# Two passes over the weights of a hybrid diffusion trunk, rewritten as one pass over all 1536 tokens

## Chip, cores, metric

The kernel runs as one program on the 8 cores of one Trainium2 chip. Every core holds the same weights and works on its own 512 context tokens (two requests of 256) and its own 1024 latent tokens (one request); nothing is exchanged between cores. The metric is the device time of the slowest core in microseconds (us).

Executions come in two states. In the slow state the cores of one die, sometimes of both, have a lower granted clock and the time is longer. (A die is four of the cores; the granted clock is the share of its full clock that TensorE was given, as the profile records it. The fast state is the one without this.) Times below are compared in the fast state, unless it says otherwise.

## The reference, cut to what matters

```python
D_MODEL = 2048; DEPTH = 2; NA_HEADS = 8; NA_HEAD_DIM = 64; D_FF = 8192

def trunk_layer(x, cond, ctx_kv, ...):
    m = jax.nn.silu(cond) @ w_ada + b_ada                 # modulation: six vectors of 2048
    sh1, sc1, g1, sh2, sc2, g2 = split(m, 6)
    h = rmsnorm(x, norm1_g) * (1 + sc1) + sh1
    q, k, v, u, vg, xf, xp, gl = split(h @ w_in)          # 7 x 512 columns, and 4 x 2048 of gates
    q = rmsnorm(q); k = rmsnorm(k)                        # per head
    a = attention                                         # context: dense, 256 keys
                                                          # latent: 8 x 16 neighbourhood + 512 cached keys
    branches = (a, spatial_gating(u, vg), fourier_mix(xf), multiscale_pool(xp))
    merged = sum_i sigmoid(gl_i + b_gate_i) * (branches[i] @ w_branch[i])
    x = x + g1 * (merged @ w_out)
    h2 = rmsnorm(x, norm2_g) * (1 + sc2) + sh2
    x = x + g2 * (square(relu(h2 @ w_mlp1)) @ w_mlp2)
# context tokens go through both layers, latent tokens go through both layers;
# they meet nowhere: the latent tokens read cached keys and values given as inputs.
```

Context and latent tokens use the same weights. A weight tile is 2048 rows by 128 columns: 1 MB in HBM as float32, 512 KB in SBUF as bf16, and 16 matmuls of 128x128 weights for each block of 512 tokens. A layer has 252 such tiles and 96 more for the modulation. Tiles are counted below as 1 MB each (504 tiles are 504 MB); the profile's HBM figures count millions of bytes, 1.05 for a tile.

## The kernel before

It runs the two groups one after the other: first the 1024 latent tokens through both layers, then the 512 context tokens. Each group loads every weight tile. The residual stays in SBUF as float32. (Cuts are marked with `...`.)

```python
    def linear(self, piece_fn, n_out, in3, in_key, NT, consumer, lookahead=1):
        for oc in range(n_out):
            bs = self.load_w(piece_fn(oc))            # one tile, DMA with a cast to bf16
            for tt in range(NT):                      # NT = 2 (latent) or 1 (context)
                bank = self.tr.bank()
                self.mm_group(self.PS[bank][:, :], bs, ...)     # 16 matmuls
                consumer(oc, tt, bank)
            self.ada_tick()
...
    def rsqrt_inplace(self, R, key):
        tr.op('act', lambda e: e.activation(out=R, in_=R, func=AF.Sqrt), ...)
        tr.op('dve', lambda e: e.reciprocal(R, R), ...)
...
        def qk_consumer(which):                       # after each projection of q and k:
                tr.op('dve', ... tensor_copy(qf[:], PS))
                tr.op('act', ... Square)
                tr.op('pe',  ... matmul(BD64, sq))    # sum over the head
                tr.op('dve', ... + EPS)
                self.rsqrt_inplace(R[:], ('sm', 1))
                tr.op('dve', ... qf * gain * R)
                tr.op('act', ... copy to bf16)
                tr.op('pe',  ... matmul(PERM, ...))   # latent: rotary
                ...                                   # three more on 'dve'
...
    def attn_latent(self, l, T, W3, B3, VL, VC, KC, TAB):
        for j in range(4):
            for hh in range(2):
                self.build_bias(l, h, TAB)            # DMA, 14 float32 matmuls, 7 VectorE instructions
                for rp4 in range(2):
                    ...                               # scores, exp, values of one head
...
    def build(self):
        self.phase0()                                 # all 96 modulation tiles of layer 0
        for gi, g in enumerate((1, 0)):               # latent, then context
            self.load_x(g, T)                         # 128x128 transposes through PSUM
            for l in range(DEPTH):
                self.norm_mod(l, g, 0, T)
                self.attention(g, l, T)
                tr.barrier()
                self.gmlp(g, l, T)
                tr.barrier()
                self.fourier(g, l, T)
                tr.barrier()
                self.pool(g, l, T)
                tr.barrier()
                self.merge(l, T)
                self.w_out_phase(l, g, T)
                self.norm_mod(l, g, 1, T)
                self.mlp(l, g, T)
            self.store_y(g, T)
```

Of the kernel before, what the change touches and what calls it, by code (L numbers as in the profile page):

```python
# [11 lines left out]
D = 2048  # L12
DEPTH = 2
# [6 lines left out]
PAST = 512  # L20
# [4 lines left out]
NDMA = 16  # L25
GELU_C = 1.5957691216057308

TRUST_SAME = ('pe',)

class Tracker:  # L30
    def __init__(self, nc):
        self.nc = nc
        self.eng = {'pe': nc.tensor, 'act': nc.scalar, 'dve': nc.vector,
                    'pool': nc.gpsimd, 'sp': nc.sync}
        self.sem = {}
        self.cnt = {}
        self.nsem = 0
        self.waited = {e: {} for e in self.eng}
        self.last_w = {}
        self.readers = {}  # L40
        for e in ('pe', 'act', 'dve', 'pool'):
            self._new_sem(e)
        self.dma_sems = [nc.alloc_semaphore(f"dq{i}") for i in range(NDMA)]
        self.dma_cnt = [0] * NDMA
        self.dma_last = [None] * NDMA
        self.dma_rr = 0
        self.dma_rr_sp = 0
        self.bank_rr = 0
        self.held = set()
        self.all_tokens = {}  # L50
# [5 lines left out]

    def epoch(self):
        for e in ('pe', 'act', 'dve', 'pool'):
            if self.cnt[e] > 0:
                self._new_sem(e)  # L60

    def bank(self, hold=False):
        for _ in range(8):
            b = self.bank_rr
            self.bank_rr = (b + 1) % 8
            if b not in self.held:
                break
        else:
            raise RuntimeError("no free PSUM bank")
        if hold:  # L70
            self.held.add(b)
        return b

    def release(self, b):
        self.held.discard(b)
# [9 lines left out]
    @staticmethod  # L85
    def _expand(keys):
        out = []
        for k in keys:
            if isinstance(k, tuple) and len(k) == 2 and k[0] == 'sm':
                out.append(('smh', k[1], 0))  # L90
                out.append(('smh', k[1], 1))
            else:
                out.append(k)
        return out

    def _deps(self, reads, writes):
        deps = []
        for k in reads:
            t = self.last_w.get(k)
            if t is not None:  # L100
                deps.append(t)
        for k in writes:
            t = self.last_w.get(k)
            if t is not None:
                deps.append(t)
            r = self.readers.get(k)
            if r:
                deps.extend(r.values())
        return deps

    def _record(self, tok, reads, writes):
        for k in reads:
            self.readers.setdefault(k, {})[tok[0].num] = tok
        for k in writes:
            self.last_w[k] = tok
            self.readers[k] = {}
        self.all_tokens[tok[0].num] = tok

    def op(self, e, fn, reads=(), writes=()):
        reads = self._expand(reads)  # L120
        writes = self._expand(writes)
        for tok in self._deps(reads, writes):
            if tok[2] == e and e in TRUST_SAME:
                continue
            self._wait(e, tok)
# [3 lines left out]
        tok = (self.sem[e], self.cnt[e], e)  # L129
        self._record(tok, reads, writes)  # L130
        return tok

    def dma(self, q, fns, reads=(), writes=()):
        reads = self._expand(reads)
        writes = self._expand(writes)
        half = NDMA // 2
        if q == 'sp':
            i = self.dma_rr_sp
            self.dma_rr_sp = (i + 1) % half
        else:  # L140
            i = half + self.dma_rr
            self.dma_rr = (self.dma_rr + 1) % half
        if self.dma_last[i] is not None:
            self._wait(q, self.dma_last[i])
        for tok in self._deps(reads, writes):
            self._wait(q, tok)
        for fn in fns:
            fn(self.eng[q]).then_inc(self.dma_sems[i], 16)
            self.dma_cnt[i] += 16
        tok = (self.dma_sems[i], self.dma_cnt[i], 'dma')  # L150
        self.dma_last[i] = tok
        self._record(tok, reads, writes)
        return tok

    def barrier(self):
        toks = list(self.all_tokens.values())
        for e in self.eng:
            for tok in toks:
                self._wait(e, tok)
        self.last_w = {}  # L160
        self.readers = {}

    def finish(self):
        for tok in list(self.all_tokens.values()):
            self._wait('sp', tok)

def _bf(x):
    return np.ascontiguousarray(x.astype(ml_dtypes.bfloat16))

def make_consts():  # L170
    c = {}
    ident = np.eye(128, dtype=np.float32)
    ones = np.ones((128, 128), np.float32)
# [4 lines left out]
    for m in range(128):  # L178
        d = m % 64
        half = (d % 32) // 16  # L180
        partner = m + 16 if half == 0 else m - 16
        perm[partner, m] = 1.0
    c['cb'] = _bf(np.concatenate([ident, ones, bd, perm], axis=1))
    jf = np.zeros((128, 64), np.float32)
    jf[np.arange(64), 63 - np.arange(64)] = 1.0
    c['cf'] = np.ascontiguousarray(np.concatenate([ident, jf], axis=1))
# [4 lines left out]
    for p in range(128):  # L191
        d = p % 64
        a = d // 32
        half = (d % 32) // 16
        i = d % 16
        ang = (pos[a] * inv[i]).astype(np.float32)
# [3 lines left out]
    qc = np.arange(64)  # L200
    cs = np.clip(qc - 8, 0, 48)
    kc = np.arange(64)
    ok = (kc[:, None] >= cs[None, :]) & (kc[:, None] < cs[None, :] + 16)
    m = np.where(ok, 0.0, NEG).astype(np.float32)
    c['mask2'] = np.concatenate([m, m], axis=0)
# [26 lines left out]

class Builder:
    def __init__(self, debug=None, depth=DEPTH, groups=(1, 0), stage=99, plan=None):
        self.stage = stage
        self.sub = 99
        self.plan = plan
        self.scopes = False
        self.ada_bg = None
        self.ada_tick_n = 0  # L240
        self.wmode = 'plain'
        self.issue_gidx = 0
        self.tile_gidx = {}
        self.rec_tiles = []
        self.rec_segs = []
        self.dma_issued = 0
        self.cast_issued = 0
        self.tile_fs = {}
        self.tile_bs = {}
        self.tile_nk = {}  # L250
        self.seg_i = 0
        self.debug = debug or []
        self.depth = depth
        self.groups = groups
# [5 lines left out]
        self.wtile_idx = 0  # L260
        self.cast_rr = 0

    def decl_dram(self):
# [3 lines left out]
        self.x_in = [di("x0", (512, D)), di("x1", (1024, D))]  # L267
        self.ck = di("ck", (DEPTH, NH, PAST, HD))
        self.cv = di("cv", (DEPTH, NH, PAST, HD))
        self.cond = di("cond", (2, D))  # L270
        self.norm1_g = di("norm1_g", (DEPTH, D))
        self.w_in = di("w_in", (DEPTH, IN_COLS // 128, 128, 2048))
        self.b_gate = di("b_gate", (DEPTH, 4 * D))
        self.q_norm_g = di("q_norm_g", (DEPTH, HD))
        self.k_norm_g = di("k_norm_g", (DEPTH, HD))
        self.rpb_pad = di("rpb_pad", (64 + DEPTH * NH * 15 * 31 + 64,))
        self.gmlp_norm_g = di("gmlp_norm_g", (DEPTH, BW))
        self.w_spatial = di("w_spatial", (DEPTH, 4, 128, 128))
        self.b_spatial = di("b_spatial", (DEPTH, 4 * 128))
        self.w_pool = di("w_pool", (DEPTH, 4, 128, 128))  # L280
        self.pool_scale = di("pool_scale", (DEPTH, BW))
        self.w_branch = di("w_branch", (DEPTH, 4, NCH, 128, 512))
        self.w_out = di("w_out", (DEPTH, NCH, 128, 2048))
        self.norm2_g = di("norm2_g", (DEPTH, D))
# [3 lines left out]
        self.b_ada = di("b_ada", (DEPTH, 6 * D))  # L288
        self.c_cb = di("cb", (128, 512), BF16)
        self.c_cf = di("cf", (128, 192))  # L290
        self.c_rope = di("rope", (128, 2, 1024))
        self.c_mask2 = di("mask2", (128, 64))
        self.c_fcc = di("f_cc", (128, 256), BF16)
        self.c_fn = [di("f_n0", (128, 2, 2, 256), BF16), di("f_n1", (128, 2, 8, 1024), BF16)]
        self.c_pm = di("pm", (128, 4, 5, 128), BF16)
        self.y_out = [do("y0", (512, D)), do("y1", (1024, D))]
        self.nk = do("nk", (2, DEPTH, NH, 256, HD))
        self.nv = do("nv", (2, DEPTH, NH, 256, HD))
        self.wcache_l = [nc.dram_tensor(f"wcache{l}", [300, 128, NCH * 128], BF16, kind="Internal").ap() for l in range(DEPTH)]
        self.dbg = {}  # L300
        for name, shape in self.debug:
            self.dbg[name] = do("dbg_" + name, shape)

    def alloc(self):
        nc = self.nc
        S = nc.alloc_sbuf_tensor
        self.XT = S("XT", [128, NCH * 1024], F32)
        self.HT = S("HT", [128, NCH * 1024], BF16)
        self.WK = S("WK", [128, NCH * 1024], BF16)
        self.BR = S("BR", [128, NCH * 1024], BF16)  # L310
# [25 lines left out]
    def psb(self, b):  # L336
        return self.PS[b][:].bitcast(BF16)
# [1102 lines left out]
```

## Time and profile before

Five runs: 7851, 7852, 7858, 7918 and, in the slow state, 8672 us. The profiled execution was in the slow state (8091 us), but only on one die: cores 0 to 3 spent about 1500 us at clock 0.81, cores 4 to 7 none, and these took 7828 to 7839 us. I read core 5, one of the undisturbed ones.

The page of core 5 of before: busy time of each engine, then tenths of busy time in 40 equal slices for TensorE (PE), its granted clock and the DMA engines, then the HBM traffic.

```profile
PE 6246.0 (80%) x33157; PEld 3025.1 (39%) x33157; DVE 1806.0 (23%) x2586; ACT 1320.3 (17%) x2201; POOL 1248.9 (16%) x1940
...
PE   1244566899799996467799979999469899579899
...
PEclk9966567999899998656999989999779999779999
DMA  9832457445345442101245524443539888359887
...
HBM read 1296.79 MB, written 16.78 MB: 168 GB/s over the span
```

The three rows show three kinds of time. In the first two slices the DMA is full and TensorE nearly idle. In others TensorE is at 4 to 7 tenths and its clock is mostly at 5 to 7: it waits, and it is cold (at half clock) for part of the time. In the rest it is full at full clock. In the full slices of the last quarter (the context pass) the DMA is nearly full too, 8 to 9 tenths.

Busy time of each engine in stretches that are stages of before, core 5. Columns: the stretch in us from the start, its length, then busy us and instruction count of TensorE, its weight loads, VectorE, ScalarE and GpSimd; granted clock, share of the DMA engines, GB/s.

```profile
core 5: us, PE busy (x) PEld busy (x) DVE busy (x) ACT busy (x) POOL busy (x), PEclk, DMA share, GB/s
0.00:331.00 331.00, 56.26 (x1541) 49.92 (x1541) 1.44 (x6) 1.51 (x2) 63.50 (x124) 1.00 0.96 154
...
445.00:1072.80 627.80, 318.97 (x3008) 224.44 (x3009) 204.20 (x336) 138.63 (x265) 52.46 (x82) 0.60 0.34 56
1072.80:1408.50 335.70, 217.21 (x1740) 115.36 (x1740) 78.37 (x116) 66.00 (x110) 43.72 (x79) 0.76 0.67 120
1408.50:1965.60 557.10, 555.86 (x2567) 251.56 (x2568) 156.07 (x229) 89.48 (x129) 68.18 (x129) 1.00 0.50 78
2075.70:2136.70 61.00, 19.17 (x46) 4.82 (x46) 30.79 (x37) 41.38 (x66) 0.25 (x1) 0.60 0.05 9
2136.70:3021.50 884.80, 884.00 (x4082) 400.05 (x4082) 96.09 (x128) 78.32 (x133) 200.38 (x256) 1.00 0.49 76
5852.10:6132.40 280.30, 278.49 (x1280) 125.64 (x1280) 77.49 (x112) 45.36 (x65) 68.18 (x129) 0.99 0.98 149
6219.90:6677.80 457.90, 447.35 (x2050) 201.27 (x2050) 48.06 (x64) 40.14 (x68) 134.77 (x192) 0.99 0.88 146
```

In order these are: the modulation of layer 0; projections and attention of the latent group in layer 0; its spatial gating, Fourier and pooling; its merge; its second norm; its MLP; and of the context pass the merge and the MLP of layer 0. The merge and MLP rows are TensorE from end to end: 4096 matmuls in 884.8 us are 216 ns for each 128x512 matmul. The Trainium skill, "TensorE: Matmul & The Clock Gate", Part 1, gives 215.7 ns for this shape warm; the trace agrees. The attention row is busy for half of its time, and at clock 0.60.

What fills the other half: the timeline of before, core 5, around one projection of q (start, length, engine and line, instruction, outputs and inputs; in brackets the idle time before it and what ended that).

```profile
561.17 0.69 DVE L680 COPY SM<-PS 128x512 f32<-128x512 f32 x1 [2.90 <-PE PS L395]
562.07 0.63 ACT L682 ACTIVATE SM<-SM 128x512 bf16<-128x512 f32 x1 [6.83 <-DVE SM L680]
562.95 0.38 PE L685 MATMUL PS<-SM,CB 128*128 128x512 bf16 x1 [1.96 <-ACT SM L682]
...
564.23 0.63 ACT L596 ACTIVATE SM<-SM 128x512 f32<-128x512 f32 x1 [1.53 <-DVE SM L687]
564.96 3.35 DVE L597 RECIPROCAL SM<-SM 128x512 f32<-128x512 f32 x1 [0.82 <-ACT SM L596]
...
570.12 0.59 PE L710 MATMUL PS<-WK,CB 128*128 128x512 bf16 x1 [6.79 <-ACT WK L693]
...
570.98 5.21 PE L395 MATMUL PS<-HT,WF 128*128 128x512 bf16 x12
```

TensorE follows VectorE and ScalarE through one chain of nine steps: the next projection's matmuls (L395) come after the rotary matmul (L710), and that waited 6.79 us. The largest single piece is the reciprocal, 3.35 us.

### The profile page before, as it was taken

How to read it: one execution, taken by the hardware profiler on the slowest of the kernel's cores; microseconds unless marked ns; L12 is line 12 of the kernel's file. 1: busy time of each engine (PE TensorE's matmuls, PEld its weight loads, DVE VectorE, ACT ScalarE, POOL GpSimd, SP SyncE). 2: the span in 40 equal slices, each digit the busy share in tenths (PEclk: the TensorE clock that was granted, in tenths of full speed). 3: DMA queues.
4: the chain of work that ended last, by engine and by line, in shares of the span. 5: the costliest groups of instructions: out<-in, count | busy, mean ns of one | idle time of the engine just before them, and what ended most of it. 6: DMA issues, size and time to landing. Idle time of an engine off the chain costs nothing.

```text
span 8089.9 us, 91572 instructions; the slowest of 8 cores (7827.5 to 8089.9 us)
## 1 busy us (share of the span) xinstructions
PE 6504.8 (80%) x33157; PEld 3086.8 (38%) x33157; DVE 1806.3 (22%) x2586; ACT 1318.8 (16%) x2201; POOL 1249.0 (15%) x1940
## 2 busy tenths in 40 slices
PE   1244556999799994477999799995698997699899
PEld 1212533444344441263444344443243442244344
DVE  0134240222211113432222211104222103222101
ACT  0121321111200012142111200002212001211100
POOL 2100011111122210000111122221021221011221
PEclk9866567999899996658999899997689987678788
DMA  9822365444344441112455355545288975278675
GB/s 150 162 52 39 60 109 114 75 78 82 54 77 76 77 75 34 15 18 52 67 76 82 53 78 76 77 69 125 49 134 135 146 124 86 47 119 135 102 124 111
DMA packets 213748, 690.37 MB, mean 85 GB/s; under 512 B 24976, under 2 KB 57856, under 8 KB 209984
## 3 DMA queue, kind: packets, MB, share of 16 engines
q0 software_dynamic: 213312, 684.52, 50.6%
q8 instruction: 278, 4.55, 0.2%
q14 instruction: 158, 1.29, 0.1%
HBM read 1296.79 MB, written 16.78 MB: 162 GB/s over the span
## 4 chain that ended last, share of the span: by engine, by line
PE 75%; DMA 7%; DVE 7%; ACT 6%; issue 3%; POOL 0%; ACTq 0%; DVEq 0%; POOLq 0%
PE PS L395 68%; DVE SM L597 2%; DMA WF<-w_ada 2%; DMA HT<-w_ada 2%; PE PS L856 1%; DMA WB<-w_ada 1%; PE PS L1134 1%; ACT WK L948 1%; DMA SM<-rpb_pad 1%; ACT HT L590 1%; DVE SM L587 1%; PE PS L958 1%; ACT SM L574 1%; PE PS L576 1%; DMA WK<-f_n 0%
## 5 line engine op out<-in xcount | busy, mean ns | idle before, releaser
L395 PE MATMUL PS<-HT,WF 128*128 128x512 bf16 x7424 | 1750.8, 398 | 45.4 <-ACT HT L590 34.4
L395 PE MATMUL PS<-HT,WB 128*128 128x512 bf16 x5632 | 1340.5, 400 | 60.4 <-ACT HT L590 34.5
L395 PEld LDWEIGHTS PS<-HT,WF 128*128 128x128 bf16 x7424 | 752.8, 102 | 1001.6 <-issue 301.5
L395 PE MATMUL PS<-WK,WF 128*128 128x512 bf16 x4000 | 902.7, 389 | 9.0 <-POOL WK L1301 4.8
L395 PEld LDWEIGHTS PS<-HT,WB 128*128 128x128 bf16 x5632 | 573.6, 102 | 794.8 <-issue 275.1
L1309 DVE SCALAR_TENSOR_TENSOR XT<-PS,MV,XT 128x512 f32<-128x512 f32 x384 | 288.3, 751 | 2536.2 <-PE PS L395 2536.2
L395 PE MATMUL PS<-WK,WB 128*128 128x512 bf16 x2896 | 656.7, 389 | 11.5 <-POOL WK L1301 9.5
L1299 ACT ACTIVATE SM<-PS 128x512 f32<-128x512 f32 x384 | 229.3, 597 | 2230.3 <-PE PS L395 2230.3
L395 PEld LDWEIGHTS PS<-WK,WF 128*128 128x128 bf16 x4000 | 398.2, 100 | 506.4 <-issue 114.2
L1301 POOL TENSOR_TENSOR WK<-SM 128x512 bf16<-128x512 f32 x384 | 396.6, 1033 | 1064.4 <-ACT SM L1299 1064.4
L395 PE MATMUL PS<-HT 128*128 128x512 bf16 x1920 | 501.0, 426 | 44.2 <-ACT HT L590 41.4
L1241 ACT ACTIVATE SM<-PS,VT 128x512 bf16<-128x512 f32 x384 | 263.9, 687 | 1454.6 <-PE PS L395 1454.5
L395 PEld LDWEIGHTS PS<-WK,WB 128*128 128x128 bf16 x2896 | 288.8, 100 | 373.1 <-issue 88.0
L1258 DVE TENSOR_TENSOR SM<-PS,SM 128x512 f32<-128x512 f32 x288 | 199.1, 691 | 948.6 <-ACT SM L1241 663.8
L395 PEld LDWEIGHTS PS<-HT 128*128 128x128 bf16 x1920 | 205.0, 107 | 326.2 <-issue 255.7
L360 POOL DMA_DIRECT2D WF<-w_mlp x236 | 131.9, 559 | 631.4 <-PE PS L395 609.5
L395 PE MATMUL PS<-WK,HT 128*128 128x512 bf16 x784 | 202.6, 427 | 4.6 <-POOL WK L1301 4.6
L574 ACT ACTIVATE SM<-XT 128x512 bf16<-128x512 f32 x192 | 112.0, 623 | 544.0 <-PE PS L576 472.8
L710 PE MATMUL PS<-WK,CB 128*128 128x512 bf16 x32 | 18.7, 585 | 217.5 <-ACT WK L693 217.5
L576 PE MATMUL PS<-SM,CB 128*128 128x512 bf16 x192 | 95.4, 522 | 121.2 <-ACT SM L574 115.7
L597 DVE RECIPROCAL SM<-SM 128x512 f32<-128x512 f32 x54 | 181.1, 3353 | 49.9 <-ACT SM L596 49.9
L395 PE MATMUL PS<-BR,WF 128*128 128x512 bf16 x772 | 192.2, 388 | 0.0
(193 smaller groups left out, 4544.6 us busy)
## 6 DMA issues: line engine op xcount, KB each, us to landing
WF<-w_mlp POOLq DMA_DIRECT2D x236, 512.0 KB, 5.6
WB<-w_mlp POOLq DMA_DIRECT2D x183, 512.0 KB, 5.7
WF<-w_in POOLq DMA_DIRECT2D x174, 512.0 KB, 5.7
WB<-w_in POOLq DMA_DIRECT2D x129, 512.0 KB, 5.3
HT<-w_mlp POOLq DMA_DIRECT2D x93, 512.0 KB, 5.6
WF<-w_ada POOLq DMA_DIRECT2D x90, 512.0 KB, 11.4
WB<-w_ada POOLq DMA_DIRECT2D x69, 512.0 KB, 10.3
HT<-w_in POOLq DMA_DIRECT2D x65, 512.0 KB, 5.9
```

Source lines behind the costliest of these rows:

```text
L360: self.tr.dma('pool', [lambda e: e.dma_start(out=wb[:, 0:nk, :], in_=src)], writes=[bkey])
L395: ins = e.matmul(out_ap, wb[:, kc, wcol], rhs_fn(kc), start=(n == 0), stop=(n == len(kcs) - 1))
L574: tr.op('act', lambda e, sq=sq, c=c: e.activation(out=sq, in_=X3[:, c, ts], func=AF.Square), reads=[('x', c, tt)], writes=[('smh', 0, c % 2)])
L576: tr.op('pe', lambda e, sq=sq, c=c: e.matmul(self.PS[bank][:, :], self.ONES, sq, start=(c == 0), stop=(c == NCH - 1)), reads=[('smh', 0, c ...
L587: tr.op('dve', lambda e, tmp=tmp, c=c, a_col=a_col: e.scalar_tensor_tensor(tmp[:], X3[:, c, ts], a_col, R[:], ALU.mult, ALU.mult), reads=[ ...
L590: tr.op('act', lambda e, tmp=tmp, c=c, b_col=b_col: e.activation(out=H3[:, c, ts], in_=tmp[:], func=AF.Identity, bias=b_col, scale=1.0), r ...
L597: tr.op('dve', lambda e: e.reciprocal(R, R), reads=[key], writes=[key])
L1241: tr.op('act', lambda e: e.activation(out=gt, in_=self.PS[bank][:, :], func=AF.Sigmoid, bias=bcol, scale=1.0), reads=[('ps', bank), 'VT'], ...
L1258: tr.op('dve', lambda e: e.tensor_tensor(tmp[:], self.PS[bank][:, :], gt, ALU.mult), reads=[('ps', bank), gk], writes=[('sm', 4)])
L1299: tr.op('act', lambda e: e.activation(out=r[:], in_=self.PS[bank][:, :], func=AF.Relu), reads=[('ps', bank)], writes=[rk])
L1301: tr.op('pool', lambda e: e.tensor_tensor(W3[:, oc, ts], r[:], r[:], ALU.mult), reads=[rk], writes=[('wk', oc, tt)])
L1309: tr.op('dve', lambda e: e.scalar_tensor_tensor(X3[:, oc, ts], self.PS[bank][:, :], gcol, X3[:, oc, ts], ALU.mult, ALU.add), reads=[('ps', ...
```

## The change

The intent: go over the weights once for all 1536 tokens (three blocks of 512); keep activations feature-major (features on partitions, tokens along the free dimension) from the input on, so that no block is transposed on TensorE; keep the residual in HBM, since three blocks of it don't fit beside the activations; compute attention for two heads at a time with keys on partitions, so that the softmax's sum comes out of the value matmul; and interleave: a small scheduler with ticks issues the next pair's projections between attention steps and runs norms behind matmuls. The bias tables are index lookups of an input and are now gathered on the host. It is a rewrite: 1172 lines added, 1261 removed. Its core, cut:

```diff
-    def barrier(self):
-        toks = list(self.all_tokens.values())
-        for e in self.eng:
-            for tok in toks:
-                self._wait(e, tok)
...
+    def w_pump(self, need=0):
+            if m >= self.w_low + NSLOT:               # ring of 8 tiles, freed in order
+                return
+            self.tr.dma('pool', self.WBT[:, off:off + 2048], src, writes=[('wb', m % NSLOT)])
...
+    def tick(self, n=1):
+            self.clock += 1
+            while self.deferred and self.deferred[0][0] <= self.clock:
+                self.deferred.pop(0)[2]()
+            for bg in list(self.bgs):                 # norms in the background
+                ...
...
-        tr.op('act', lambda e: e.activation(out=R, in_=R, func=AF.Sqrt), reads=[key], writes=[key])
-        tr.op('dve', lambda e: e.reciprocal(R, R), reads=[key], writes=[key])
+            self.act(R.ap, self.PS[b2][:, :], AF.Ln, [('ps', b2), 'EPS'], [R], bias=self.EPSC)
+            self.act(R.ap, R.ap, AF.Exp, [R], [R], scale=-0.5)
...
+    def fill(j):                                      # what runs between the steps of pair j
+            if j < 3:
+                yield from self.qk_all(l, j + 1, DB)
+            t = self.w(self.w_in[l, 20 + j])          # a quarter of the Fourier projection
+            ...
+        for n in range(N + 2):
+            if n >= 2:
+                values(n - 2)
+            if n < N:
+                scores(n)
+                want = -(-(n - i0 + 1) * tot // nj)
+                while done < want:
+                    next(filler, None)                # 8 matmuls
+                    done += 1
+                    self.tick()
...
+    def one(oc, tt, t):                               # output projection
+            bank = self.bank()
+            self.run(self.group(self.PS[bank][:, :], bank, self.fm(t, self.W3, tt)))
+            x = self.x2(oc, tt)                       # loaded from HBM three tiles ahead
+            self.stt(x.ap, self.PS[bank][:, :], g, x.ap, ALU.mult, ALU.add, ...)
+            tr.dma('sp', self.xa[l][tt, oc], x.ap, ...)
+            self.stat(x, banks[tt], oc, 2)            # sum of squares for the next norm
...
     def build(self):
+        self.phase0()                                 # 32 modulation tiles, not 96
+        for l in range(DEPTH):
+            self.stage_a(l)                           # gating, first pair's q and k, v
+            self.attention(l)
+            self.stage_b(l)                           # Fourier, pooling
+            if l == 0:
+                self.ada_begin(0, [((32, 16),), ((48, 16),), ((64, 16),)])
+            self.merge(l)
+            self.project_out(l)
+            if l == 0:
+                self.ada_begin(0, [((80, 16),)])
+                self.ada_begin(1, [((16 * k, 16),) for k in range(6)])
+            self.mlp(l)
```

## The prediction

It was written from before's profile and the code, with nothing built.

> **What bounds the kernel now.** I read the undisturbed die (core list: cores 4 to 7, 7828 to 7839 us, no throttle; the other die spent about 1500 us at clock 0.81). Busy times by stage (core 5) show two regimes.
>
> - Dense stages are at TensorE's pace: the latent merge (1408-1964 us) is 554.5 of 556 us busy, the two MLP quarters-loops (2140-3020, 4600-5483 us) 880 of 880: one 128x512 matmul per 216.6 ns at clock 1.00. The context pass (5700 on) is at the same pace while its DMA share is 0.86 to 0.89: it reads a 1 MB weight tile for only 16 matmuls (3.47 us).
> - Elsewhere TensorE waits. First 331 us: 96 modulation tiles, DMA share 0.96, TensorE busy 56 us. Loading x and norm, 109 us; each later norm about 62 us (busy 22). Query/key/value 312 us (busy 140), latent attention 320 and 235 us, clock 0.50. The clock record has about 1850 us at half clock.
>
> **The sum after.** The linear layers keep their count: per layer and 512 tokens 252 weight tiles x 16 = 4032 matmuls, so 24192 in all x 216.6 ns = 5240 us. This is the floor and does not shrink. Other TensorE work, from columns at the pace of the dense stages (estimates): attention 126, Fourier 72, norm sums 42, pooling, spatial and query/key helpers 50, modulation 192 tiles x 0.53 us = 100. Sum 5630 us.
>
> Waits that stay (estimates):
> - start: 32 modulation tiles instead of 96, at 3.4 us each, plus x: 135 us, then 20 us while the norms of the latent blocks catch up;
> - attention: per head pair, ScalarE has 40 exponentials x 0.61 us + 20 us of query/key norm and finish = 44 us, VectorE 36, TensorE 49 incl. the next pair's projections: I expect 62-66 us, the last pair about 40, so 135 us of waits in both layers;
> - query/key helpers not covered by one chunk 24; norm sums issued slightly early 30; stage changes and Fourier/pool 60.
>
> 5630 + 135 + 20 + 135 + 24 + 30 + 60 = about 6035 us at clock 1.00; a little throttle gives **6110 us** (ratio 1.29). Gone: barriers, transposes, the 3.35 us reciprocals (54 + 12, now Ln/Exp), 500 MB of the weight reads (HBM read 1297 to about 810 MB; residual traffic adds 100). The gain is mostly idle and cold time, not bytes: the halved weight traffic frees only the start of the context pass, which was hardly slower than TensorE.
>
> **Clock.** The Trainium skill, "TensorE: Matmul & The Clock Gate", Part 1, says that idle windows halve the clock and that three busy cores of a die can bring 13/16. This trace has both: 0.50 in attention, 0.81 on die 0. Filling gaps should end most cold time; denser work can trip the second more often. A throttle over a quarter of the run costs some 300 us, over all of it 1200.
>
> **Range** 5880 to 6600 us. Faster by over 2%: 0.97; within: 0.02; slower: 0.01.
>
> **What would show it.** TensorE busy over 93%; half clock under 400 us; matmul count near 27500 + 3072 small ones; stages: merge 835 us, MLP 1335 us per layer, attention 230 us per layer, dense work starting at 150 us; DMA share well under 0.6 after the start; HBM read about 800 MB.
>
> **What would make it wrong.** A 0.81 clock through the whole run; ScalarE table loads between Ln and softmax Exp (the skill's "ScalarE: Activation LUTs", Table sets, puts both in one set, so I expect few loads; each took 1.28 us here); attention running at over 90 us per pair because in-order ScalarE and VectorE queues block the two score banks; weight DMAs stuck behind a waiting load on the same queue.

## More of the kernel before

The chain of waits of before, core 5, at the start of one head of attention (start, length, what it was):

```profile
797.37 0.48 POOL SM L847
798.08 7.49 DMA SM<-rpb_pad
805.81 5.43 PE PS L856 x25
...
812.20 0.62 DVE BR L860
```

This is layer 0. Each of its 8 heads begins with its bias table: a DMA of 7.5 to 10.3 us during which neither TensorE, VectorE nor ScalarE works, then float32 matmuls of 5.4 us. The DMA engines are at 0.90 in that stretch: modulation tiles of layer 1 are loading at the same time. In layer 1, where no modulation tiles pass, only the first head waits for this DMA (4.4 us), the others for the matmuls alone; a head takes 27 us there and 38 us in layer 0. That the modulation tiles make the difference was not tested.

## The result

Five runs: 6038, 6039, 6039, 6047 and, in the slow state, 6348 us; the median is 6039.4. In the same rounds before had a median of 7857.8. The ratio is 0.7676 (95% interval 0.7637 to 0.7715). Ratios are computed as the mean time of one kernel's fast runs over that of the other's fast runs of the same rounds, so they are not quite the ratio of the medians. The output was correct.

The page of core 7 of after, the slowest core of a fast execution, with the same rows as above:

```profile
PE 5699.3 (94%) x29080; PEld 2582.4 (43%) x29080; DVE 1428.7 (24%) x2172; ACT 1194.6 (20%) x1929; POOL 383.1 (6%) x722
...
PE   1788999999999999999999889999999999999999
...
PEclk9899999999999999999999999999999999999999
DMA  9522144443656578656765221222236334543353
...
HBM read 861.59 MB, written 79.69 MB: 156 GB/s over the span
```

The low patches of TensorE and of its clock are gone, except at the start. The clock record sums to 109 us at half clock on this core (93 to 229 on all eight) against 1841 to 1881 us before.

Busy time in the stages of layer 0 of after, core 7, columns as in before's stages: start; gating, first q and k, and v; attention; Fourier and pooling; merge; output projection; MLP.

```profile
core 7: us, PE busy (x) PEld busy (x) DVE busy (x) ACT busy (x) POOL busy (x), PEclk, DMA share, GB/s
0.00:159.40 159.40, 29.64 (x540) 19.12 (x541) 13.40 (x34) 28.95 (x45) 21.47 (x44) 1.00 0.96 178
159.40:354.50 195.10, 165.49 (x750) 72.95 (x750) 70.54 (x111) 84.88 (x132) 13.76 (x23) 0.91 0.39 77
354.50:598.00 243.50, 195.32 (x894) 72.87 (x894) 110.33 (x189) 145.55 (x260) 6.41 (x13) 0.99 0.30 73
598.00:691.50 93.50, 90.16 (x534) 47.47 (x534) 22.54 (x33) 24.47 (x43) 2.11 (x4) 0.98 0.19 44
691.50:1575.00 883.50, 857.60 (x4612) 398.65 (x4611) 224.56 (x341) 133.21 (x193) 67.14 (x128) 0.99 0.42 76
1575.00:1770.00 195.00, 183.68 (x818) 76.52 (x816) 55.57 (x78) 51.89 (x80) 8.71 (x17) 1.00 0.63 170
1770.00:3131.00 1361.00, 1353.61 (x7818) 634.16 (x7816) 215.65 (x315) 156.02 (x258) 124.93 (x237) 1.00 0.65 128
```

Adding such rows over both layers, and for before over both groups, shows where the time came from. The cuts are at the first instructions of each stage.

| stage | before, core 5, us | after, core 7, us |
|---|---|---|
| start: modulation, loading x, first norm of each layer in each pass (and storing y) | 634 | 159 |
| mixers: projections, attention, gating, Fourier, pooling | 2328 (TensorE busy 1357) | 1080 (TensorE busy 933) |
| merge | 1675 | 1717 |
| output projection | 335 | 392 |
| second norm | 181 | 0 |
| MLP | 2685 | 2690 |
| sum | 7838 | 6038 |

The dense stages (merge, output projection, MLP) did not get shorter: 4695 us before, 4799 after. They now carry 160 modulation tiles of 0.53 us and the sums of the norms. The whole gain is in the start, the mixers and the norms. In the mixers, TensorE's waiting fell from 971 to 147 us and its busy time by 424 us: fewer small matmuls and transposes, and hardly any work at half clock; these are not told apart. Over the whole span, TensorE's waiting fell from 1593 to 339 us and its busy time from 6246 to 5699 us, so about 1254 of the 1800 us are waits.

### The profile page after: what moved, and what is told of

Same layout as the page of the kernel before. It is cut to its first block, busy times and chain, and to the rows that moved or that the text cites. A ratio compares the mean times of both kernels' runs of the same rounds, so it can differ in the third digit from the quotient of the medians.

```text
span 6038.4 us, 76841 instructions; the slowest of 8 cores (6011.1 to 6038.4 us)
## 1 busy us (share of the span) xinstructions
PE 5699.3 (94%) x29080; PEld 2582.4 (43%) x29080; DVE 1428.7 (24%) x2172; ACT 1194.6 (20%) x1929; POOL 383.1 (6%) x722
## 4 chain that ended last, share of the span: by engine, by line
PE 86%; DMA 4%; ACT 4%; DVE 3%; issue 2%; SPq 1%; POOL 0%; DVEq 0%; ACTq 0%; POOLq 0%
PE PS L424 81%; DMA WB<-w_in 2%; ACT EX L455 2%; DVE HB L460 2%; PE PS L494 1%; ACT HB L455 1%; PE PS L532 1%; DMA WB<-w_ada 1%; DMA WK<-x 1%; PE PS L846 1%; PE PS L891 1%; DVE EX L460 1%; SPq L137 1%; DMA WB<-w_branch 0%; ACT HB L457 0%
## 5 line engine op out<-in xcount | busy, mean ns | idle before, releaser
L424 PE MATMUL PS<-HB,WB 128*128 128x512 bf16 x15360 | 3373.3, 380 | 19.9 <-DMA WB<-w_in 9.7
L424 PEld LDWEIGHTS PS<-HB,WB 128*128 128x128 bf16 x15360 | 1490.7, 98 | 1819.6 <-issue 65.2
L424 PE MATMUL PS<-WK,WB 128*128 128x512 bf16 x7680 | 1684.8, 379 | 0.4 <-DVE MV L463 0.4
L424 PEld LDWEIGHTS PS<-WK,WB 128*128 128x128 bf16 x7680 | 746.5, 98 | 883.0 <-issue 2.7
L455 ACT ACTIVATE EX<-PS 128x512 f32<-128x512 f32 (+1 forms) x432 | 257.3, 596 | 1771.1 <-PE PS L424 1753.2
L463 DVE TENSOR_TENSOR EX<-PS,EX 128x512 f32<-128x512 f32 x408 | 280.9, 688 | 1272.5 <-ACT EX L457 1138.5
L457 ACT ACTIVATE EX<-PS,VT 128x512 bf16<-128x512 f32 x384 | 263.9, 687 | 1442.5 <-PE PS L424 1442.5
L463 DVE TENSOR_TENSOR HB<-EX 128x512 bf16<-128x512 f32 x384 | 265.6, 692 | 1063.5 <-ACT EX L455 1063.5
L460 DVE SCALAR_TENSOR_TENSOR EX<-PS,MV,EX 128x512 f32<-128x512 f32 x192 | 144.2, 751 | 1197.3 <-PE PS L424 1190.8
L424 PE MATMUL PS<-WB,HB 128*128 128x512 bf16 x1152 | 271.4, 394 | 23.1 <-DMA WB<-w_in 11.6
```

Source lines behind the costliest of these rows:

```text
L424: ins = e.matmul(out, lt, rh, start=(i0 + k == 0), stop=(i0 + k == n - 1))
L455: self.tr.op('act', lambda e: e.activation(out=out, in_=in_, func=func, scale=scale), reads, writes)
L457: self.tr.op('act', lambda e: e.activation(out=out, in_=in_, func=func, bias=bias, scale=scale), reads, writes)
L460: self.tr.op('dve', lambda e: e.scalar_tensor_tensor(out, in0, sc, in1, op0, op1), reads, writes)
L463: self.tr.op('dve', lambda e: e.tensor_tensor(out, in0, in1, op), reads, writes)
```

## The experiments

Theory: the time is TensorE's work at 216 ns per matmul plus the gaps in which TensorE waits for chains on ScalarE, VectorE and single DMAs. The change wins by filling the gaps. Rival: the name of the change says "one pass over the weights"; the 504 MB of weight reads that it saves made it faster. A narrower rival for each part: that it is hidden behind something else, so that undoing it costs nothing.

### Before, with few bytes in the context pass

The second pass over the weights is kept, but each of its tiles loads one eighth of its bytes (`cur_g` is 0 in the context pass). The results are wrong.

```diff
+        if self.cur_g == 0:
+            nk, src = 2, src[:, 0:2, :]
         self.tr.dma('pool', [lambda e: e.dma_start(out=wb[:, 0:nk, :], in_=src)], writes=[bkey])
```

> The kernel before, in which the context pass loads one eighth of each weight tile (its results are wrong on purpose): the 504 MB of the second pass over the weights become 63. Theory (bytes were not the limit): the context pass, 2355 us of the undisturbed die, gets at most 120 us shorter, where its merge and MLP waited for tiles; whole kernel 7730 to 7820. Rival (the second pass over the weights is what the change saved): at least 600 us faster, under 7250.

Measured: fast runs 7839 to 7930 us against 7844 to 7888 of before; ratio 1.004 (0.993 to 1.015). HBM reads fell to 847 MB, less than after's 862. The context merge and MLP of layer 0 in this kernel, core 5 (the same stages as the last two rows of before's table above, same columns):

```profile
5840.00:6120.00 280.00, 278.01 (x1283) 125.67 (x1282) 77.51 (x112) 45.29 (x65) 67.89 (x129) 1.00 0.27 31
6206.00:6662.00 456.00, 445.45 (x2049) 200.59 (x2047) 48.07 (x64) 40.62 (x68) 134.90 (x192) 0.99 0.16 19
```

The DMA share fell from 0.98 and 0.88 to 0.27 and 0.16, and the stages stayed at 280 and 456 to 458 us. The cores of the undisturbed die took 7819 to 7825 us against 7828 to 7839: some 12 us. Removing all of the bytes that the change saves (450 MB here, 435 there) gains almost nothing. The time missed my range (7730 to 7820) on the side away from the rival: I had expected a gain of 30 us or more. A DMA share of 0.98 did not mean that TensorE waited for the DMA: it was busy 278.5 of 280.3 us with it, and 278.0 of 280.0 without.

### After, with the weights read twice

The reverse: every tile but the modulation's is read once more, as a copy inside HBM.

```diff
             self.tr.dma('pool', self.WBT[:, off:off + 2048], src, writes=[('wb', m % NSLOT)])
+            if twice:
+                self.tr.dma('pool', self.dum[m % 4], src, writes=[('dum', m % 4)])
```

> The kernel after, in which every weight tile but the modulation's is read from HBM a second time, into a dummy in HBM that nobody reads. HBM reads go to about 1365 MB, more than the 1297 of before. Theory (the time is TensorE's work plus the gaps in which it waits for the vector engines; bytes were not the limit): at most 60 us slower than after, 6040 to 6100, the matmul pace stays 216 ns. Rival (the halved weight reads made it faster): at least 300 us slower, over 6340, with TensorE waiting for weight DMAs in the MLP and merge stages.

Measured: fast runs 6415 and 6420 us, ratio 0.8183 (0.8159 to 0.8207): 380 us slower than after. By the totals the rival's number came out. My range for the theory (6040 to 6100) was missed by over 300 us. The stages say where: up to the attention of layer 1 the trace of core 0 shows 3692 us against 3338, so 354 us in layer 0 and the way to layer 1; from there to the end 2726 against 2700 us. In layer 1 the merge (829 us) and the MLP (1329 us) are as long as in after, with twice their reads. Layer 0 is also the place of the 160 later modulation tiles, and in its MLP the DMA share came to 0.97. My edit also overshot: the copies wrote 264 MB to HBM, so the traffic (1390 MB read, 344 MB written) was well over before's (1297 and 17). So it showed that there is a ceiling, not that after is at it. A cleaner form was needed.

### After, with layer 1's weights read twice

Now the second read goes into the tile's own slot, nothing is written to HBM, and only layer 1, which has no modulation tiles, does it: 252 MB, what before read for its second pass of this layer.

```diff
+            if self.last is not None:
+                n, psrc = self.last                   # the tile issued just before
+                self.tr.dma('pool', self.WBT[:, off:off + 2048], psrc, writes=[('wb', n % NSLOT)])
```

> The kernel after, in which every weight tile of layer 1 is read a second time into its own slot of the ring, 252 MB more, which is what the kernel before read for layer 1's second pass; nothing is written to HBM. In the earlier run that doubled all tiles with a copy inside HBM, layer 0 lost about 330 us where modulation tiles, doubled tiles and the residual met, while the merge and the MLP of layer 1 stayed at 840 and 1329 us. Theory: at most 40 us slower than after, 6040 to 6080, all of it in layer 1's output projection. Rival (the second reads cost their DMA time): 252 MB at the 304 GB/s of the start would be 830 us of DMA time, and at least 150 us of it would show.

Measured: one fast run of six, 6079.8 us (the others 6209 to 6746, slow), 41 us more than after's 6039; four of its cores took 6036 to 6044 us, the other four 6067 to 6079. On core 0 layer 1's part from attention on took 2719 us against 2700, and its MLP stayed at 1329 us. The MLP of layer 1, first after, core 7, then this kernel, core 0 (columns as above):

```profile
4709.00:6038.00 1329.00, 1325.12 (x6139) 600.42 (x6137) 217.92 (x308) 129.12 (x215) 63.41 (x120) 1.00 0.42 87
4749.00:6078.00 1329.00, 1318.76 (x6017) 600.43 (x6138) 218.14 (x308) 129.40 (x215) 127.93 (x241) 1.00 0.65 135
```

The second reads cost 41 us at most, against some 870 us of DMA time that they take (an estimate, from the 96 tiles in 331 us of before's start; the 830 of the expectation counts a tile as exactly a million bytes). That is just over the edge that I wrote, and not all of it lies in the output projection as I had said (11 to 13 us do, 8 are in the merge, and 20 us more show in the move from layer 0 to layer 1, where the residual is read back). With one fast run on another chip the last 20 us are not firm. With this run and the one with few bytes, the rival is out where it was tested: the second pass's bytes did not make before slow, and a second read would cost little in layer 1 of after. A clean second read in layer 0, beside the 160 later modulation tiles, was not run. By an estimate from the same 331 us, its MLP would need 1270 us of DMA time (2 x 128 + 112 tiles) of its 1361. So the halved reads may be what leaves room for moving the modulation; this stays open.

### Before, with Ln and Exp in place of Sqrt and reciprocal

```diff
-        tr.op('act', lambda e: e.activation(out=R, in_=R, func=AF.Sqrt), reads=[key], writes=[key])
-        tr.op('dve', lambda e: e.reciprocal(R, R), reads=[key], writes=[key])
+        tr.op('act', lambda e: e.activation(out=R, in_=R, func=AF.Ln), reads=[key], writes=[key])
+        tr.op('act', lambda e: e.activation(out=R, in_=R, func=AF.Exp, scale=-0.5), reads=[key], writes=[key])
```

> The kernel before, with Ln and Exp on ScalarE in place of Sqrt on ScalarE and the 3.35 us reciprocal on VectorE, in its 66 norms; nothing else. Theory (before runs these chains one at a time, so their length is on the chain): about 2.7 us less for each, 110 to 180 us faster, 7670 to 7740. Rival (hidden behind matmuls of the other group): under 40 us faster.

Measured: correct; fast runs 7654 and 7661 us against 7844: 187 us faster, a little over my range. That is 2.8 us for each of the 66 norms. In the traces Sqrt (0.63 us) and the reciprocal (3.35 us) became Ln and Exp of 0.63 us each, 2.72 us less, and there are 18 table loads (of ScalarE's function tables, 1.28 us each) instead of 22: together 185 us. So as good as nothing of these chains was hidden. This part alone, two lines, is a tenth of the gain.

### Before, with one bias table per layer

```diff
-                self.build_bias(l, h, TAB)
+                if h == 0:
+                    self.build_bias(l, h, TAB)
```

> The kernel before, with the bias table built for the first head of each layer only (attention results are wrong on purpose). Theory: the build is not overlapped; a head takes 38 us in layer 0 and 27 us in layer 1 and about 15 us without it, so 14 builds less are 200 to 260 us faster, about 7620. Rival (the build runs beside the previous head): under 60 us faster.

Measured: fast runs 7660 to 7663 us against 7844, ratio 0.9748 (0.9698 to 0.9799): about 184 us faster. The theory holds; the size is just under my range, because a head without its table takes about 19 us (by subtraction: 32.5 on average, less 184/14), not 15. The tables were wrong.

### Before, with both

The two edits together.

> The kernel before with Ln and Exp for the norms and with one bias table per layer, together (attention results wrong on purpose). Alone they gave 195 and 190 us. Theory (every chain of before stands alone between waits, so parts add up): about 385 us, 7460 to 7480. Rival (both shorten the same wait): nearer to 7650.

Measured: fast runs 7481 to 7504 us against 7845 to 7862, ratio 0.9541 (0.9516 to 0.9566): about 360 us from the means, just short of the range that I wrote. Alone they gave 187 and 184 (195 and 190 in the expectation). They add up, nearly: the two chains do not hide each other.

### After, with all modulation tiles first

```diff
+        self.ada_begin(0, [((32, 16),), ((48, 16),), ((64, 16),), ((80, 16),)])
+        while self.ada_step():
+            pass
         self.bg_done.add(('n1', 0))
```

(The later requests for these 64 tiles are taken out.)

> The kernel after, with all 96 modulation tiles of layer 0 computed before the first projection, as before. Theory: at the start each of the 64 more tiles costs its DMA time, 3.4 us, so 218 us more at the start; given back are 0.53 us of TensorE time for each later and the 26 us of waits in the merge of layer 0; in all about 160 us slower, 6200 (6170 to 6260). Rival (the DMAs of the later tiles were not hidden either): no change, under 40 us.

Measured: fast runs 6197, 6202 and 6220 us; 158 us slower by the best. The first projection starts at 363 us instead of 152, so 211 us later; the merge of layer 0 is 48 us shorter (first to last sigmoid) without its 48 tiles. Both sides of the sum came out as written. Moving 64 tiles of 3.4 us from a place where TensorE waits for them to one where it does not is worth 158 us.

### After, with the filler in front

The same instructions; the next pair's projections, with the norm steps that they put off (`flush`), run before the pair's attention steps and not between them.

```diff
                 filler, done, i0 = fill(cur), 0, n
-                next(filler)
+                for _ in filler:
+                    self.tick()
+                self.flush()
```

> The kernel after, in which the next pair's projections run before the attention steps of a pair instead of between them. Same instructions, other order. Theory (interleaving hides ScalarE's and VectorE's time of the softmax behind matmuls): the first three pairs go from 66 to about 85 us, the last from 46 to about 50, and TensorE's clock falls to 0.5 in the attention steps; in both layers 130 us slower (90 to 180), about 6170. Rival (the new attention is fast because it needs less work of each engine; the order is worth little): under 40 us slower.

Measured: correct; one fast run of five, 6124.6 us, 85 us slower than after. That is under my range (90 to 180) and over the rival's 40. Busy time of the pairs of layer 0 in this kernel, core 7 (columns as in the stage rows above):

```profile
352.10:428.60 76.50, 64.37 (x241) 21.69 (x240) 29.75 (x50) 38.56 (x67) 1.59 (x3) 0.82 0.37 71
428.60:510.30 81.70, 68.70 (x253) 22.87 (x251) 31.09 (x52) 40.93 (x71) 1.58 (x3) 0.77 0.18 42
...
590.70:642.00 51.30, 40.94 (x147) 12.40 (x146) 18.45 (x33) 28.04 (x51) 1.06 (x2) 0.73 0.35 106
```

The same pairs in after, core 7, with the same columns:

```profile
354.50:420.00 65.50, 53.71 (x248) 20.35 (x248) 30.13 (x52) 37.89 (x67) 2.18 (x5) 1.00 0.37 76
420.00:486.00 66.00, 53.55 (x248) 20.37 (x248) 30.36 (x52) 39.49 (x71) 1.58 (x3) 1.00 0.21 52
...
552.00:598.00 46.00, 34.15 (x148) 11.66 (x148) 19.21 (x36) 28.33 (x52) 1.05 (x2) 0.96 0.48 129
```

With the filler in front a pair takes 76 to 82 us instead of 66. TensorE's busy time itself rises from 54 to 64 to 69 us, because its clock falls from 1.00 to about 0.8: gaps are paid for twice. The interleaving is worth 85 us, 5% of the gain, by this one fast run; most of what the new attention saves does not come from the order.

### After, with two waits moved

After's trace shows 48 us of TensorE waiting just before the norm's sum matmul of q and k (L647), and 26 us of waits in the merge of layer 0, 23 of them before weight tiles (the expectation counts all 26). In after's timeline, core 7, the sum matmul, matmuls of the values, and then the norm's Ln and Exp:

```profile
441.01 0.68 DVE L463 TENSOR_TENSOR EX<-EX,WK 128x512 f32<-128x512 f32 x1
441.24 0.38 PE L647 MATMUL PS<-HB,CB 128*128 128x512 bf16 x1 [1.01 <-DVE EX L463]
441.45 0.59 PE L891 MATMUL PS<-HB,WK 128*128 128x512 bf16 x2
441.71 0.69 ACT L457 ACTIVATE EX<-PS,SMALL 128x512 f32<-128x512 f32 x1 [1.01 <-PE PS L647]
...
442.49 0.63 ACT L455 ACTIVATE EX<-EX 128x512 f32<-128x512 f32 x1
```

The second wait comes, as I read the code, from the ring of weight tiles, which frees slots in order. The branch tile is the second of eight tiles of a round of the merge and is held to the round's end, so the next round's branch tile and those behind it are requested only then.

```diff
-            self.defer(2, pm)
-        self.defer(1, bd)
+            self.defer(3, pm)
+        self.defer(2, bd)
...
-                    if i < 3:
+                    if i in (0, 2):
                         self.ada_tick()
...
             self.w_free(t)                            # in the output projection
+            if l == 0:
+                self.ada_tick()
...
```

> The kernel after, with two small moves: the query/key norm's sum matmul is issued one chunk of 8 matmuls later (and the rotary matmul one more tick later), and a third of the modulation tiles moves from the merge of layer 0 to the output projection. The trace of after shows 48 us of TensorE waiting before the norm's sum matmul and 26 us before weight tiles in that merge. Theory: both waits are on the chain, so 60 us faster (35 to 85), about 5980. Rival (they hide other waits that then show, above all ScalarE in attention): under 20 us.

Measured: fast runs 6042, 6048 and 6048 us: no gain. The rival was right for the first move. The matmul L647 no longer waits, and others do (timeline of this kernel, core 6):

```profile
443.15 0.38 PE L647 MATMUL PS<-HB,CB 128*128 128x512 bf16 x1
443.37 0.59 PE L891 MATMUL PS<-HB,WK 128*128 128x512 bf16 x2
...
447.26 0.59 PE L666 MATMUL PS<-WK,CB 128*128 128x512 bf16 x1 [2.58 <-DVE EX L460]
```

The norm's Ln and Exp now stand in ScalarE's queue behind the softmax's exponentials, VectorE waits for them (57 us in the attention of layer 0, against 21 in after), and TensorE waits at the rotary matmul (L666) and at the value matmuls (L891). Attention rose from 243.5 to 256.6 us. The wait was not removed; waits further down the same chain grew by more than it.

### After, with the modulation tiles spread alone

The second move without the first.

> The kernel after, with only the second move of the earlier run that had two: 15 of the 48 modulation tiles go from the merge of layer 0 to the output projection. In that run the merge of layer 0 fell from 888 to 867 us while attention rose by 13 us in each layer, so this part alone should give 15 to 25 us, about 6018. If the sum stays at 6040, the tiles' waits have only moved to the output projection.

Measured: correct; fast runs 6026 and 6029 us; ratio 0.7670 (0.7611 to 0.7728), so by the ratio alone not different from after's 0.7676, and 12 us where I had expected 15 to 25. It was run again beside the unchanged kernel on one chip.

> The kernel after, unchanged, on the chip of the next two runs, for a comparison there. Expected 6038 to 6050 in the fast state.

> The kernel after with 15 modulation tiles moved from the merge of layer 0 to the output projection, on the same chip as the unchanged one. The earlier run gave 6025.7. Theory (the weight waits of that merge were on the chain): 10 to 20 us faster than the unchanged one in fast runs. Rival (the earlier difference was chance between chips): within 4 us.

Measured: the unchanged kernel had one fast run of eleven, 6038.7 us; the spread one 6027.1 and 6028.4 us of six (ratio to before 0.7677, 0.7655 to 0.7700). The difference is 11 to 12 us both times, and the trace has it where it should be: the merge of layer 0 is 17 us shorter (first to last sigmoid 860 against 877 us), the output projection 4 us longer. So this wait was on the chain; most of the 23 us went. This version is faster than both kernels, by 0.2% over after: too little for the intervals, enough for the trace.

## Why the prediction was right

Predicted 6110 us (5880 to 6600), of which 6035 at full clock; measured 6039, with the fast executions at full clock but for 93 to 229 us. That the sum of 6035 hit so closely is luck: TensorE's work was 69 us more than written and the waits 66 us less. Point by point:

- **Floor.** Written: 24192 matmuls at 216.6 ns, 5240 us. The trace has just these 15360 + 7680 + 1152 matmuls in the groups of the linear layers, and the MLP and the merge of layer 1 took 1329 and 834 us (written: 1335 and 835; in layer 0, with the later modulation tiles, they took 1361 and 884). TensorE's busy time was 5699 us (written: 5630).
- **Waits.** Written: 405 us. Measured: 339 us (span less busy time). The terms compare as follows. Start 135 and 20: 130 us, and 30 in the first mixer stage of layer 0. Attention 135: 95, in pairs of 66 and 46 us (written 62 to 66 and 40). Norm sums 30: 22 us in the two output projections and 12 in the MLP stages. Stage changes with Fourier and pooling 60: 7. Query/key helpers outside of attention 24: under 10, within 16 us of waits in the first mixer stage of layer 1, most of which stand before norm sums. Not foreseen at all: 28 us in the two merges, 26 of it before weight tiles. The sum was good because errors of tens of us had both signs, and because all of it is 6% of the span.
- **"The gain is mostly idle and cold time, not bytes."** Not bytes: shown, but for the open end in layer 0. Taking the second pass's bytes away from before gains 12 us of 1800; giving layer 1 its second reads back costs 41 at most. Mostly idle: 1254 of the 1800 us are TensorE's waits. How the other 547 us divide between cold time and work left out was not measured. The sentence that the smaller traffic "frees only the start of the context pass" named an even larger effect than there was.
- **Clock.** Half clock 93 to 229 us (written: under 400). In the profiled fast execution no core had any time at 0.81. The slow state takes more from this kernel than from before: in eleven runs on one chip, ten were slow, 6314 to 7095 us, up to 17% longer; before's slow runs there went up to 8737 us, 11%. The profile of a slow one has about 2300 of 6400 us at 0.81 on one die. That four of the five runs of the result were fast is luck too; the median of those eleven is 6549 us. The allowance of 75 us for "a little throttle" was the main error of the point estimate.
- **Table loads.** 20 of 1.28 us each, 22 before. The Trainium skill, "ScalarE: Activation LUTs", Table sets, says that one set holds Exp and Ln; the trace agrees, since Ln and Exp alternate in attention without a load between them.
- **Wrong in detail.** The small matmuls were counted too high (27500 written for all but the modulation's 3072, 29080 less 3072 = 26008 measured). Attention took 244 and 249 us, not 230. HBM reads were 862 MB, not 810. The DMA share was not "well under 0.6" everywhere: it was 0.63 to 0.65 in the output projection and the MLP of layer 0, and the second reads of the experiment brought that MLP to the ceiling (0.97, with the copies' writes to HBM).

How the gain of 1800 us divides is known in part. Runs of single parts: norms by Ln and Exp 187 us, bias tables 184, modulation spread 158, interleaving 85; these were measured on different kernels, so their sum (614) is a guide only. The second norms behind matmuls are 181 us by the stage table (their reciprocals are in the 187 as well). The rest, some 1000 us, was not taken apart. What else changed is feature-major activations without transposes, two heads at a time, keys on partitions, and stages without barriers; which of these gave how much is not shown. Before without its barriers, the plainest test of one part, was not run. That stays open.

## What to carry to other kernels

Split the span into stages and ask of each whether TensorE is full at full clock; if it is, only fewer matmuls help there, and a DMA share of 0.98 beside it cost next to nothing here. Where it is not full, see whether the length of each chain of small steps is on the critical path instruction by instruction, as it was here; then shorten it (2.8 us for each norm here), move work that nobody waits for into the dense stages, and put independent matmuls between the steps, which also keeps the clock up. A wait that is moved along the same chain is not removed; check in the trace which engine's queue it went to.

## What the Trainium skill lacked or had wrong

- "TensorE: Matmul & The Clock Gate", Part 1 (the note on the peak-current limiter), says that on the default power profile a die goes to 13/16 of the clock within 5 to 20 us of a third core starting dense matmuls and stays there while the load lasts. Here all eight cores ran dense matmuls together, and the profiled fast execution of after had no time at 0.81 in 6039 us (that of the spread version had 4 us, on two cores). In a slow one, one die had about 2300 us at 0.81 and the other none. It comes and goes between executions of one kernel. Which power profile this chip has is not on record.
- The same page, Part 2 (Back-to-back issue gap), gives about 131 ns per matmul at N=512 as the sustained pace in a stream with weight loads. This case's streams, with a weight load before each matmul, ran at 216 ns (4096 in 884.8 us), which is the page's own figure for the isolated gap.
- "Trainium Kernel Development and Optimization", Performance Expectations, calls matmul busy time a bad metric for the distance to the roofline. Alone it was bad here too: it rose from 54 to 69 us for the same work when the clock fell to 0.77. What that section lacks is that busy time is of use beside the granted clock: busy 884.0 of 884.8 us at clock 1.00, at 216 ns for each matmul, marked a stage at the matmuls' own pace; like stages took as long with an eighth of the bytes (280 us) or with twice the reads (1329 us).
- No page that I read gives the time of VectorE's float32 reciprocal: 3.35 us for 128x512, against 0.69 to 0.75 us for other VectorE instructions of this shape; Ln and Exp on ScalarE took 0.63 to 0.69 us each.
